# Other estimated times in the planner of a streaming encoder layer (attention and delta rule with two chains)

## The chip, the cores and the metric

The kernel runs on one core of a Trainium2 chip. The time is the device time of one execution in microseconds (us), the median of several runs. The core has a matrix engine (TensorE, PE in the profile, with its weight loads PEld), a vector engine (VectorE, DVE), an engine for functions of one argument (ScalarE, ACT), a general engine (GpSimd, POOL) and SyncE (SP), which issues the DMAs of this kernel. Each engine works off a queue of its own strictly in the order in which the program put instructions there. Engines tell each other of results through semaphores; an instruction whose input is not there yet holds up all that stands behind it in its queue.

## The reference

One layer of an encoder, for a prompt of 2048 frames and for a sample of 32 frames with caches. The width is 1024. In short:

```python
hp = layer_norm(x_prompt); hs = layer_norm(x_sample)
qa, ka, va, za, qkv_b, zb, a_b, b_b, gate_a, gate_b = split(h @ w_in)     # 1024 -> 6160 columns
# branch A: 8 heads of 64, softmax attention over the own chunk of 64 frames and the 8 before it, bias by distance
ya = (attention(qa, ka, va, rel_bias) * silu(za)) @ w_branch_a
# branch B: 8 heads of 64, depthwise causal conv of width 4 + silu on q, k, v; q and k of unit length
g, beta = -exp(a_log) * softplus(a_b + dt_bias), sigmoid(b_b)
for each chunk of 64 frames:                                              # chunked delta rule, float32
    m = (k * beta) @ k.T * decay * strictly_lower
    t_inv = inverse(eye + m);  u = t_inv @ (v * beta);  w = t_inv @ (k * beta * exp(gc))
    v_new = u - w @ s                                                     # s: state, 64 x 64 per head
    o = (q * exp(gc)) @ s + (q @ k.T * decay) @ v_new
    s = s * exp(g_last) + k_dec.T @ v_new
yb = (rms_norm(o) * silu(zb)) @ w_branch_b
y = layer_norm(ALPHA * h + (sigmoid(gate_a) * ya + sigmoid(gate_b) * yb) @ w_out)
```

Results are both outputs, the newest keys and values, the last rows before the conv, and the states.

## The kernel before, in words

**Stages.** The prompt is worked off in two halves of 1024 frames, the sample with the second. For each half the kernel runs a delta-rule phase (`phase_b`, line 776) and then an attention phase (`phase_a`, line 1425). After the second attention phase comes the merge (`merge`, line 2036) with the two branch projections, the output projection and the last norm.

**Projections.** The input projection is cut into 48 jobs of 128 columns, plus one for the decay inputs, once per half. A list (`all_jobs`, line 1907) fixes their order. `divide` (line 613) splits weights into two f16 parts (`whi`, `wlo`: ScalarE and GpSimd), and `multiply` (line 657) issues 24 matmuls for each block of up to 512 frames into one of two PSUM banks (`pj`). Each block is then evacuated by ScalarE or VectorE to where its phase wants it: `raw` for the conv of the delta rule, `vf`, `rhi`, `zs` for attention, `sig` (through `sig_dram`) for the merge gates. Merge-gate jobs depend on no phase. They stand between the others: `HEAD`, `FILL` and `TAIL` (lines 50 to 55) say how many at the start of a half, between the delta-rule jobs, and after them. Jobs of attention wait until their phase has been entered, and that happens once the delta-rule phase before it is done.

**The delta rule.** A block is eight chunks of two heads; a half has eight blocks (four pairs of heads, two blocks each), and the second half has one more for the sample. For each block there are the conv (VectorE, ScalarE), the decay matrices (`prep`), the system (`system`: products of keys and queries), the solution by forward substitution (`substitute`, line 1229: for each of 31 columns VectorE multiplies into `sys_t` and subtracts from `sys_u`), the inverse, and then the chain (`chain`, line 1305). The chain goes over the chunks one after the other because of the state. One chunk's step is: TensorE multiplies the state (`x`), VectorE forms `r`, TensorE multiplies by the inverse, VectorE forms `vn`, TensorE multiplies by the keys, VectorE forms the new `state`; two more matmuls make the output `o`. Every pair of heads has a chain of its own, and two of them can be under way at once (`x_banks = places(2)`, line 1291). `tail` (line 1337) norms the output and writes `gb` (`gs` for the sample).

**The planner.** Nothing of this is ordered by hand. Each piece of work is a Python generator, a stream, with a clock of its own, and `Flow` (line 155) always continues the stream whose clock is the earliest. When a stream issues an instruction, `Engine` (line 218) puts it in the engine's queue at once, asks `price` (line 224) for its estimated time, and `spend` (line 191) sets the stream's clock to

```python
t = max(t, self.busy.get(key, 0.0)) + cost
self.busy[key] = s.clock = t
```

where the first `t` is the clock plus a hop between engines (`HOP_PE, HOP, HOP_SAME = 0.1, 0.2, 0.12`, line 53: into TensorE, into another engine, and from an engine to itself). Buffers and banks are handed over through gates, at the planned clock, and the issue of DMAs has its place by the same clock. So the estimates decide the order of instructions in every queue, and nothing else: on the chip an instruction takes what it takes.

In `price`, key `"PE"` is TensorE, `"V"` VectorE, `"S"` ScalarE, `"G"` GpSimd; `n` is the number of elements per partition, `far` says that an operand lies in PSUM, and `more` counts operands that are themselves tensors of one value per partition. In the trace nearly all instructions stand at line 259, the helper that issues them, so the prediction goes by tiles.

Of the kernel before, what the change touches and what calls it, by code (L numbers as in the profile page):

```python
# [210 lines left out]
def width(ap):  # L211
    n = 1
    for k in ap.shape[1:]:
        n *= k
    return n


class Engine:
# [5 lines left out]
    def price(self, name, a, k):  # L224

        if self.key == "PE":
            n, m = width(a[2]), width(a[1])
            if name == "transpose":
                n = m = max(a[1].shape[0], m)
            if a[1].dtype == F16:  # L230
                return max(n / 2400.0, m / 4800.0)
            if a[1].dtype == F32R:
                return n / 2400.0
            return max(n, m) / (1200.0 if name == "transpose" else 600.0)
        ins = [k[x] for x in ("in_", "in0", "in1") if x in k] or list(a[1:2])
        out = k["out"] if "out" in k else a[0]
        n = width(ins[0] if name in ("bn_stats", "tensor_reduce") else out)
        far = any(getattr(x, "space", None) == PSUM for x in ins + [out])
        if self.key == "G":
            if k.get("op") == ALU.pow:  # L240
                return 0.55 + 0.125 * n
            return 0.03 + n / 1200.0 if name == "memset" else 0.1 + n / (960.0 if name == "affine_select" else 480.0)
        more = sum(not isinstance(k.get(x, 0.0), (int, float, type(None)))
                   for x in ("scale", "bias", "accum_out", "scalar1", "scalar2"))
        if self.key == "S":

            table = k.get("func") == AF.Ln
            if "func" in k and table != self.table and k["func"] != AF.Copy:
                self.table = table
                return 1.28 + self.price(name, a, k)  # L250
            return (0.05 if far else 0.093) + 0.093 * more + n / 1200.0
        fast = name in ("tensor_copy", "tensor_scalar") and not far
        return (0.125 if far else 0.068) + 0.06 * more * fast + n / (1920.0 if fast else 960.0)

    def __getattr__(self, name):
        f = getattr(self.eng, name)
# [2038 lines left out]
```

## Time and profile before

| | us |
|---|---|
| median of 3 runs | 2121.21 (2118.57 to 2124.31) |
| the profiled execution | 2124.96 |
| its span | 2123.1 |
| mean granted TensorE clock | 0.98 |

A row of a group names the tiles it writes and reads (`r<-x,negc,v_t`), shapes, the count, then the busy time, the mean of one instruction in ns, and the idle time of its engine just before. A row of the timeline starts with the time from the span's start and the duration. A row of the waits names who waited, for whom, and the total, the number and the longest. Where a plain float32 matmul is counted, the trace holds two records for each (264 of `x<-r,u_bd` for 132 of `r`). Matmuls overlap one another, so the record of one is longer than its share of the engine.

### The profile page before, as it was taken

Reading aid. Unit: us, or ns where it says so; the run is one execution under the profiler, and the core shown is the slowest. Engines: PE = TensorE matmul, PEld = TensorE weight load, DVE = VectorE, ACT = ScalarE, POOL = GpSimd, SP = SyncE. Lnnn points to the kernel's source line nnn. Section 1 sums busy time; section 2 is a strip of 40 time slices with the busy share of each in tenths; the row PEclk is TensorE's granted clock in tenths of the full one; section 3 lists DMA queues with packets and bytes.
Section 4 is the critical chain, followed back from the end, with each engine's and each line's share of the span. In section 5 each row is a group of like instructions: output and inputs, shape, how many; then the busy total and the mean of one; then the engine's idle time right before and its main releaser. Section 6 shows DMA issues by size and latency. Waiting matters only on the chain. (4 is left out here: it accounts for less than half of the span.)

```text
span 2123.1 us, 41363 instructions
## 1 busy us (share of the span) xinstructions
PE 1994.4 (94%) x15098; PEld 1422.5 (67%) x15098; DVE 1534.2 (72%) x4660; ACT 978.7 (46%) x2098; POOL 634.3 (30%) x708
## 2 busy tenths in 40 slices
PE   4999898999999999999899999999999988999998
PEld 4454665666465656666666676767776777988896
DVE  7689989884277768779898987347657667766676
ACT  5655544443465667564444443346656652111110
POOL 6243333232322122333233232310110223443343
PEclk9999999899999999999999999999999999999999
DMA  3223232222423233222223233332322435443331
GB/s 120 75 84 102 76 88 78 67 79 82 122 67 120 82 93 99 70 73 76 58 70 94 62 86 85 99 100 72 92 77 67 138 120 191 128 123 103 116 107 61
DMA packets 197719, 196.49 MB, mean 93 GB/s; under 512 B 79622, under 2 KB 147570, under 8 KB 197516
## 3 DMA queue, kind: packets, MB, share of 16 engines
q1 hardware_dynamic: 197516, 193.85, 30.9%
q8 instruction: 119, 1.95, 0.4%
q14 instruction: 84, 0.69, 0.1%
HBM read 135.91 MB, written 50.53 MB: 88 GB/s over the span
## 5 line engine op out<-in xcount | busy, mean ns | idle before, releaser
L259 PE MATMUL pj<-hi,whi 128*128 128x512 f16 (+2 forms) x1992 | 650.7, 342 | 8.6 <-POOL whi L259 3.0
L259 PE MATMUL pj<-hi,wlo 128*128 128x512 f16 (+2 forms) x1952 | 640.8, 341 | 0.4 <-POOL wlo L259 0.4
L259 PEld LDWEIGHTS <-whi 128*128 128x128 f16 x3984 | 416.0, 106 | 217.5 <-issue 11.2
L259 PE MATMUL pj<-lo,whi 128*128 128x512 f16 (+2 forms) x1992 | 461.9, 340 | 0.0
L259 POOL TENSOR_TENSOR wlo<-wraw,whi 128x512 f16<-128x512 f32 x192 | 228.6, 1193 | 630.1 <-ACT whi L259 345.1
L259 PEld LDWEIGHTS <-wlo 128*128 128x128 f16 x1952 | 205.5, 105 | 108.5 <-issue 8.9
L259 ACT CAST mh<-sg 128x256 fp32r<-128x256 f32 x64 | 25.9, 407 | 276.1 <-DVE sg L259 276.0
L259 DVE TENSOR_TENSOR sys_u<-sys_u,sys_t 128x60 f32<-128x60 f32 (+24 forms) x527 | 135.7, 258 | 18.2
L259 PE MATMUL a<-ghi,whi 128*128 128x256 f32 (+1 forms) x512 | 134.8, 293 | 7.1 <-DVE sg L259 6.8
L259 ACT ACTIVATE wraw<-wraw,w_scale 128x1024 f32<-128x1024 f32 (+1 forms) x98 | 111.4, 1137 | 59.2 <-DVE w_scale L259 57.1
L259 ACT CAST ph<-b 128x512 f16<-128x512 f32 (+2 forms) x224 | 92.6, 422 | 92.7 <-PE b L259 86.1
L259 PE MATMUL a<-ghi,wlo 128*128 128x256 f32 (+1 forms) x512 | 131.9, 287 | 0.0
L259 ACT CAST whi<-wraw 128x512 f16<-128x512 f32 (+1 forms) x196 | 119.4, 611 | 27.1 <-PE pj L259 24.2
L259 DVE TENSOR_TENSOR pl<-b,ph 128x512 f16<-128x512 f32 (+2 forms) x224 | 107.6, 484 | 28.9 <-ACT ph L259 28.0
L259 DVE TENSOR_TENSOR sys_t<-sys_u,sys_p 128x54 f32<-128x54 f32 (+21 forms) x459 | 123.6, 269 | 4.0
L259 ACT ACTIVATE sb<-sb,mx,unit 128x640 f32<-128x640 f32 (+4 forms) x128 | 109.0, 852 | 25.5 <-DVE mx L259 25.1
L259 DVE SCALAR_TENSOR_TENSOR acc<-raw,cwT,acc 128x512 f32<-128x512 f32 x144 | 113.2, 786 | 8.4 <-ACT acc L259 7.4
L259 POOL TENSOR_TENSOR w_scale<-w_scale,mhalf 128x1 f32<-128x1 f32 x49 | 31.0, 633 | 288.0 <-DVE w_scale L259 230.1
L259 PEld LDWEIGHTS a<-ghi,whi 128*128 128x128 f32 x512 | 99.3, 194 | 8.8 <-DVE sg L259 7.9
L259 PE MATMUL b<-ident,sb 128*128 128x128 f32 x560 | 98.8, 276 | 2.9 <-ACT tmp L259 0.6
L259 ACT COPY v_t<-o 128x64 f32<-128x64 f32 x132 | 27.5, 209 | 158.3 <-PE o L259 121.5
L259 PEld LDWEIGHTS a<-ghi,wlo 128*128 128x128 f32 x512 | 98.9, 193 | 0.4 <-DVE wlo L259 0.2
(350 smaller groups left out, 4238.9 us busy)
## 6 DMA issues: line engine op xcount, KB each, us to landing
wraw<-in_w_in SPq DMA_DIRECT2D x192, 256.0 KB
sg<-sig SPq DMA_DIRECT2D x112, 128.0 KB
sig<-sig SPq DMA_DIRECT2D x44, 256.0 KB
sys_p<-sol_p SPq DMA_DIRECT2D x17, 512.0 KB
x<-in_x_p SPq DMA_DIRECT2D x16, 512.0 KB
xt<-in_x_p SPq DMA_DIRECT2D x16, 512.0 KB
out_y_p<-xt SPq DMA_DIRECT2D x16, 512.0 KB
glo<-g SPq DMA_DIRECT2D x14, 512.0 KB
```

Source lines behind the costliest of these rows:

```text
L259: r = f(*a, **k)
```

## The change

The arithmetic of `price` is changed, and only that. On VectorE, ScalarE and GpSimd the constant part of every estimate grows: by 0.040 us, 0.050 us and 0.120 us (powers on GpSimd stay). On TensorE, f16 matmuls get a floor and a small constant, float32r matmuls a lower rate, plain float32 matmuls one fixed time (by the number of partitions of the stationary operand), and float32 transposes one of two fixed times. The hops, the DMA estimates, the job list and all instructions stay. The streams are therefore continued in another order, and the queues of all engines, SyncE's with its DMAs among them, get the same instructions in another order.

```diff
             if a[1].dtype == F16:
-                return max(n / 2400.0, m / 4800.0)
+                return max(0.029, n / 2400.0 + 0.0025)
             if a[1].dtype == F32R:
-                return n / 2400.0
-            return max(n, m) / (1200.0 if name == "transpose" else 600.0)
+                return n / 2265.0
+            if name == "transpose":
+                return 0.109 if n > 64 else 0.06
+            return 0.165 if a[1].shape[0] > 32 else 0.07
...
-            return 0.03 + n / 1200.0 if name == "memset" else 0.1 + n / (960.0 if name == "affine_select" else 480.0)
+            return 0.150 + n / 1200.0 if name == "memset" else 0.220 + n / (960.0 if name == "affine_select" else 480.0)
...
-            return (0.05 if far else 0.093) + 0.093 * more + n / 1200.0
+            return (0.100 if far else 0.143) + 0.093 * more + n / 1200.0
         fast = name in ("tensor_copy", "tensor_scalar") and not far
-        return (0.125 if far else 0.068) + 0.06 * more * fast + n / (1920.0 if fast else 960.0)
+        return (0.165 if far else 0.108) + 0.06 * more * fast + n / (1920.0 if fast else 960.0)
```

## The prediction

> **What bounds the kernel now.** I read the page first: engines, then the slices (40 equal pieces of the span, busy share in tenths).
>
> ```profile
> PE 1994.4 (94%) x15098; PEld 1422.5 (67%) x15098; DVE 1534.2 (72%) x4660; ACT 978.7 (46%) x2098; POOL 634.3 (30%) x708
> ...
> PE   4999898999999999999899999999999988999998
> ...
> DVE  7689989884277768779898987347657667766676
> ```
>
> TensorE is busy 94% of the span; 128.7 us are left (2123.1 - 1994.4). In the two stretches where VectorE's digits are mostly 8 and 9, the delta-rule phases (one per half of the prompt), TensorE's show 8 among the 9. The windows view cuts these stretches out, and others; its columns are length, then busy us (instructions) of PE, weight loads, DVE, ACT, POOL, then granted clock, DMA share, GB/s.
>
> ```profile
> 200.00:450.00 250.00, 230.44 (x1728) 156.40 (x1726) 222.49 (x782) 117.65 (x247) 83.11 (x110) 0.95 0.29 79
> 450.00:551.00 101.00, 98.64 (x688) 61.71 (x687) 47.12 (x194) 41.45 (x86) 31.61 (x30) 1.00 0.32 93
> 1000.00:1275.00 275.00, 250.97 (x2180) 187.37 (x2179) 243.20 (x845) 122.08 (x279) 85.51 (x124) 0.99 0.29 75
> 1275.00:1383.00 108.00, 103.89 (x839) 73.64 (x838) 53.78 (x219) 36.72 (x86) 28.85 (x26) 0.97 0.33 94
> ...
> 1710.00:1800.00 90.00, 76.86 (x549) 65.88 (x548) 64.14 (x131) 31.29 (x70) 29.17 (x25) 0.92 0.50 159
> ...
> 0.00:100.00 100.00, 68.28 (x402) 42.60 (x403) 70.07 (x175) 58.41 (x105) 44.71 (x56) 0.95 0.27 93
> ...
> 1500.00:1600.00 100.00, 98.53 (x921) 71.28 (x919) 64.17 (x232) 60.28 (x141) 11.58 (x10) 1.00 0.30 86
> ...
> 1800.00:1900.00 100.00, 100.00 (x666) 91.97 (x665) 70.01 (x114) 12.95 (x35) 44.16 (x33) 1.00 0.40 123
> ```
>
> Rows one and three are the heavy parts of the delta rule: VectorE busy 89% and 88%, TensorE 92% and 91%. Rows two and four are the ends of these phases: VectorE falls to 47% and 50%, and gate projections keep TensorE at 98% and 96%. Then the entry to the merge (13.1 us of TensorE idle), the start (31.7 us), attention (1.5 us in 100) and the merge (none).
>
> The view of waits, for the chain of the delta rule (r, vn and state are VectorE's three results of one chunk's step; columns: us in total, times, longest):
>
> ```profile
> PEld x L259 <- DVE r L259: 40.2, 82, 1.8
> PEld x L259 <- DVE vn L259: 36.1, 63, 1.8
> ...
> PEld x L259 <- DVE state L259: 21.4, 42, 2.6
> ```
>
> TensorE's queue comes to the next link of the chain before VectorE has delivered it: 187 waits, 97.7 us, 0.52 us each. A part is covered by matmuls in flight; behind each waiting weight load stands all the rest of TensorE's queue. Only another order can change these waits, and the diff changes orders.
>
> One more reading, the slack behind each delta-rule phase. Its end must come before the next attention phase's projections may leave PSUM; until then TensorE works off gate projections. VectorE's last outputs of the two phases (gb, gs) and ScalarE's first evacuations of attention (vf), from the timeline:
>
> ```profile
> 536.48 0.88 DVE L259 SCALAR_TENSOR_TENSOR gb<-b,gz,gb 128x256 f32<-128x256 f32 x2
> ...
> 550.83 0.69 ACT L259 ACTIVATE vf<-pj,w_inv 128x512 f32<-128x512 f32 x1 [0.97 <-PE pj L259]
> ...
> 1362.32 0.70 DVE L259 TENSOR_SCALAR gs<-gs,w_inv 64x32 f32<-64x32 f32 x4
> ...
> 1383.05 0.69 ACT L259 ACTIVATE vf<-pj,w_inv 128x512 f32<-128x512 f32 x1 [3.60 <-PE pj L259]
> ```
>
> From the end of gb (537.4) to 550.8 are 13.5 us, from the end of gs (1363.0) to 1383.05 are 20.0 us: together 33.5 us by which TensorE's waits may shrink before the end of the chain, and no longer TensorE, sets when attention starts.
>
> **The change part by part.** No instruction is added, removed or resized, so each engine's busy time stays. What moves is each queue's order, through the planner's clock.
>
> VectorE: every price rises by 0.040 us. Two neighbours with nothing in the way, two neighbours on ScalarE, and a case with GpSimd at work:
>
> ```profile
> 1346.37 0.28 DVE L259 TENSOR_SCALAR vn<-x,sc 128x64 f32<-128x64 f32 x1
> 1346.56 0.35 DVE L259 TENSOR_TENSOR ms<-ms 128x8 f32<-128x8 f32 x2
> ...
> 1367.71 0.48 ACT L259 ACTIVATE sig<-pj,w_half 128x272 f32<-128x272 f32 x1
> 1368.09 0.61 ACT L259 CAST whi<-wraw 128x512 f16<-128x512 f32 x1
> ...
> 355.23 1.04 POOL L259 TENSOR_TENSOR v_t<-v_t,ms 128x512 f32<-128x512 f32 x1 [0.16 <-DVE sys_t L259]
> 355.27 1.05 DVE L259 TENSOR_TENSOR sys_u<-sys_u,sys_t 128x30 f32<-128x30 f32 x1
> ...
> L259 DVE TENSOR_TENSOR sys_u<-sys_u,sys_t x527: 173/218/1214, 142.5 to 1323.9; 128x60 f32<-128x60 f32 x17, 128x28 f32<-128x28 f32 x14, 128x66 f32<-128x66 f32 x12, 128x48 f32<-128x48 f32 x11
> ...
> L259 DVE TENSOR_TENSOR sys_u<-sys_u,sys_t 128x60 f32<-128x60 f32 (+24 forms) x527 | 135.7, 258 | 18.2
> ```
>
> vn (64 columns from PSUM) holds VectorE for 0.19 us although its record is 0.28 us long. The old price is 0.125 + 64/960 = 0.192, the new one 0.232. So the old price is the spacing of undisturbed neighbours, and the new one lies between spacing and record. But sys_u, whose median record is 218 ns, takes 1.05 us beside a GpSimd instruction of 1.04 us, and its mean is 258 ns: 40 ns above the median, just what the diff adds. The new price is thus about the mean cost with such disturbances, spread evenly.
>
> The Trainium skill (Perfetto Trace Analysis, Optimizing Scalar/DVE Operations) gives about 60 ns (125 ns with PSUM) as VectorE's engine-busy overhead per instruction and 93 and 51 ns for ScalarE, and says that profiled latency is about twice that because half of it overlaps with the next instruction; vn agrees (0.19 against 0.28). By this rule the diff charges for time in which the engine is free, and the sum would come out slower; that is the second rival.
>
> ScalarE: +0.050 us. sig leaves after 0.38 us; old 0.05 + 0.093 + 272/1200 = 0.370, new 0.420. I cost this at nothing: in the heavy parts ScalarE is busy 47% and 44%, and its evacuations run beside the other bank's matmuls. Without that cover, (247 + 279) x 0.05 = 26 us of planned work would count. GpSimd: +0.120 us, 33% and 31% busy there, nothing likewise; 234 x 0.12 = 28 us uncovered.
>
> TensorE: f16 matmuls of 512 columns go from 0.213 to 0.216, float32r from 0.107 to 0.113 (256) and 0.213 to 0.226 (512). The merge's pieces of the chain that ended last give the true ones:
>
> ```profile
> 1833.78 22.81 PE a L259 x192
> ...
> 1862.38 5.45 PE b L259 x24
> ```
>
> 22.81/192 = 0.119 and 5.45/24 = 0.227: both new prices are nearer. But TensorE has no idle time in the merge, so a better estimate has nothing to remove there; the same holds for attention. The start I also take as unchanged: 0. Plain float32 matmuls of the chain fall from 0.213 to 0.165. What a round trip is really worth stands at the end of the first phase, where the chain runs alone on VectorE:
>
> ```profile
> 515.12 0.28 DVE L259 SCALAR_TENSOR_TENSOR r<-x,negc,v_t 128x64 f32<-128x64 f32 x1 [0.53 <-PE x L259]
> 515.93 0.28 DVE L259 TENSOR_SCALAR vn<-x,sc 128x64 f32<-128x64 f32 x1 [0.53 <-PE x L259]
> 516.75 0.28 DVE L259 SCALAR_TENSOR_TENSOR state<-state,sc,x 128x64 f32<-128x64 f32 x1 [0.53 <-PE x L259]
> ...
> L259 DVE SCALAR_TENSOR_TENSOR r<-x,negc,v_t 128x64 f32<-128x64 f32 x132 | 36.9, 279 | 25.5 <-PE x L259 23.8
> ```
>
> 0.81 us from one VectorE link to the next. The plan's round trip is hop 0.1 + matmul + hop 0.2 + VectorE: old 0.1 + 0.213 + 0.2 + 0.192 = 0.705, new 0.1 + 0.165 + 0.2 + 0.232 = 0.697. The unloaded chain is not repaired: 0.008 us worse. What is repaired is its queueing. The four delta-rule rows hold 782 + 194 + 845 + 219 = 2040 VectorE instructions; 132 chunk steps of three links are 396 of them, so 1644/396 = 4.15 others stand per link, and the plan's link comes up to 4.15 x 0.04 = 0.166 us later when all of them are ahead of it. Then TensorE's queue has that much other work before it reaches the link. Ends: none ahead, 187 waits x (-0.008) = 1.5 us lost; all ahead, 187 x (0.166 - 0.008) = 29.5 us won. I take half of them ahead (a link becomes ready at any point between its neighbours): 187 x (0.083 - 0.008) = 14 us. That is under the 33.5 us of slack, so it reaches the end.
>
> SyncE's queue is written by the same clock: a load issued behind a DMA that waits for a late result is late too. The longest waits of this kind now:
>
> ```profile
> POOL ms L259 <- DMA gb<-z: 15.4, 1, 15.4
> ...
> POOL wlo L259 <- DMA qd<-rhi: 13.0, 1, 13.0
> ```
>
> Both fall on GpSimd, which is idle 70% of the span; 0 in the sum, 15 us either way as its bound.
>
> Sum: the profiled execution took 2124.96 us (span 2123.1 and 1.9 around it). 2124.96 - 14 = 2111. It lay 3.75 us above the median of the runs shown (2121.21), so for the median I forecast **2107 us**.
>
> **The rivals.** First, the order hardly changes what happens: conv, delta-rule and gate projections come in a fixed list and wait for fixed numbers of buffers, and the unloaded round trip moves by 0.008 us. For it: VectorE at 89% sets the pace of the heavy parts whatever TensorE's order. Against it: the 187 waits are waits of order. Time 2121.
>
> Second, slower: the plan overcharges VectorE where it is fullest. Place: the heavy parts. Price: 782 x 0.04 = 31 us and 845 x 0.04 = 34 us by which the planned chain ends later, with gate projections set ahead of its links; the real TensorE then keeps the links back while VectorE idles. It decides where the chain's end comes later by more than the slack, 13.5 and 20.0 us; then TensorE has no gates left and idles until attention opens. At full price (31.3 - 13.5) + (33.8 - 20.0) = 31.6 us, at the point itself 0; the middle is 16: 2137. The rows of vn and sig speak for it, the mean of sys_u against it. It is what the skill's rule on overlapped overhead (same section) would bring about.
>
> Third, slower at one place: the entry to the merge (13.1 us of TensorE idle in 90) loses as much again, since there VectorE, GpSimd and half-busy DMA engines feed new weights in an order of their own: 2134. Against it: the prices there become truer.
>
> Fourth, a larger gain: links also come sooner for VectorE. Its idle time in the heavy parts is 27.5 + 31.8 = 59.3 us; half of that and the 14: 2121.2 - 44 = 2077. It needs the phases themselves to shorten.
>
> **How the numbers follow.** 0.3% is 6.4 us, about what a measurement of this kernel can tell from no change. Chances: forecast 0.40 (own range 2092 to 2123 by its two ends; 0.34 of it below 2114.8), no change 0.18, overcharge 0.25, merge entry 0.08, larger gain 0.09. Faster 0.34 + 0.09 = 0.43, same 0.06 + 0.18 = 0.24, slower 0.33. The range takes in the larger gain and most of the overcharge (full price 2153): 2074 to 2148.
>
> **What would show it.** Right: the three chain waits of TensorE's weight loads together well below 97.7 us (about 60 or less); VectorE's busy time and counts as before; TensorE idle in the heavy rows below 44 us (19.6 + 24.0 now); the slack behind each phase smaller than 13.5 and 20.0 but above zero; a lone round trip still 0.81 us. Wrong: chain waits as long as before (first rival); TensorE idle between the last gate projection and the first vf, with gb or gs ending later than now (second); the fifth row below 77 us of TensorE per 90 (third); VectorE above 92% in the heavy parts (fourth).

## The result, and the profile after

The changed kernel takes 2145.52 us (median of 4 runs, 2144.23 to 2152.01) against 2120.32 us before in the same comparison: a ratio of 1.0126 with a 95% interval of 1.011 to 1.0142. It is 25 us **slower**; I had forecast 2107, faster by 14. The profiled execution took 2152.01 us, 6.5 us above its median, with a span of 2149.8.

First the page of the changed kernel: engines, then the slices of TensorE and of its granted clock (tenths).

```profile
PE 2002.5 (93%) x15098; PEld 1451.1 (67%) x15098; DVE 1534.6 (71%) x4660; ACT 975.8 (45%) x2098; POOL 640.8 (30%) x708
...
PE   4999999999899998997999999899999998999998
...
PEclk8999999899899999999999999699999999999999
```

Counts are the same and VectorE's busy time is (1534.6 against 1534.2). TensorE's busy time grew by 8.1 us with the same 15098 matmuls, while its mean granted clock fell from 0.98 to 0.96, and one slice stands at 6. The waits of the chain, which were 187 and 97.7 us:

```profile
PEld x L261 <- DVE r L261: 26.7, 48, 3.1
...
PEld x L261 <- DVE vn L261: 19.3, 31, 1.7
...
PEld x L261 <- DVE state L261: 8.5, 24, 0.8
```

They are 103 and 54.5 us. What I forecast of TensorE's waits came about, and the time still rose. To see where it went, I cut both spans at the same events: ScalarE's first evacuation of the decay inputs (`ab`) of each half, its first evacuation of attention (`vf`) of each half, and the end of attention's last output (`ga`). So the rows are start, first delta rule, first attention, second delta rule, second attention, merge. The windows view of before:

```profile
0.00:75.40 75.40, 44.65 (x240) 31.12 (x241) 52.82 (x138) 37.47 (x75) 35.85 (x43) 0.93 0.29 102
75.40:550.80 475.40, 446.90 (x3087) 279.12 (x3086) 373.97 (x1252) 236.28 (x456) 163.92 (x205) 0.97 0.30 85
550.80:883.00 332.20, 325.36 (x2492) 199.46 (x2491) 228.03 (x777) 208.65 (x436) 78.06 (x85) 0.99 0.31 93
883.00:1383.00 500.00, 465.33 (x3818) 334.16 (x3817) 387.50 (x1296) 229.10 (x491) 155.09 (x214) 0.98 0.29 78
1383.00:1736.00 353.00, 344.03 (x3207) 249.09 (x3205) 224.82 (x780) 210.75 (x494) 50.59 (x44) 1.00 0.31 89
1736.00:2123.10 387.10, 368.18 (x2264) 329.51 (x2262) 267.03 (x418) 56.40 (x146) 150.82 (x119) 0.98 0.39 123
```

And of the changed kernel:

```profile
0.00:79.30 79.30, 47.46 (x240) 31.73 (x241) 52.21 (x138) 36.75 (x76) 35.88 (x43) 0.89 0.28 97
79.30:548.00 468.70, 443.21 (x3107) 285.80 (x3105) 369.24 (x1249) 240.30 (x462) 162.03 (x202) 0.96 0.30 85
548.00:889.40 341.40, 323.40 (x2469) 201.67 (x2470) 230.24 (x781) 203.09 (x430) 82.50 (x87) 0.98 0.31 91
889.40:1395.00 505.60, 472.35 (x3836) 352.12 (x3834) 384.84 (x1287) 228.77 (x493) 152.68 (x208) 0.94 0.27 75
1395.00:1761.00 366.00, 345.23 (x3154) 247.03 (x3154) 227.82 (x785) 211.11 (x495) 56.42 (x50) 0.98 0.30 88
1761.00:2149.80 388.80, 370.81 (x2295) 332.76 (x2295) 270.23 (x422) 55.79 (x147) 151.25 (x120) 0.98 0.38 122
```

The differences are +3.9, -6.7, +9.2, +5.6, +13.0 and +1.7 us, together the 26.7 us of the spans. The two delta-rule phases, on which my whole sum rested, come out level (-1.1 us). **Attention, which I had put at zero, is 22.2 us longer**, with 18.0 and 20.8 us of TensorE idle instead of 6.8 and 9.0.

How the delta-rule phases ended in the changed kernel (last gate evacuation `sig`, first evacuation of attention `vf`, VectorE's last outputs `gb` and `gs`):

```profile
525.35 0.69 ACT L261 ACTIVATE sig<-pj,w_half 128x512 f32<-128x512 f32 x1
...
548.01 1.26 ACT L261 ACTIVATE vf<-pj,w_inv 128x512 f32<-128x512 f32 x2
...
554.42 0.88 DVE L261 SCALAR_TENSOR_TENSOR gb<-b,gz,gb 128x256 f32<-128x256 f32 x2 [2.40 <-PE b L261]
...
1354.68 0.49 ACT L261 ACTIVATE sig<-pj,w_half 128x272 f32<-128x272 f32 x1
...
1391.97 0.70 DVE L261 TENSOR_SCALAR gs<-gs,w_inv 64x32 f32<-64x32 f32 x4
...
1394.98 1.05 ACT L261 ACTIVATE vf<-pj,w_inv 128x512 f32<-128x512 f32 x2
...
1400.85 0.88 DVE L261 SCALAR_TENSOR_TENSOR gb<-b,gz,gb 128x256 f32<-128x256 f32 x2 [2.27 <-PE b L261]
```

`gb` of the first phase and `gs` of the second end 17.9 us (555.3 against 537.4) and 29.7 us (1392.7 against 1363.0) later. In the second phase the last prompt block now ends behind the sample: its `gb` ends at 1401.7 us, where that of before ended at 1356.0. The gates are used up 22 and 40 us before attention begins. And attention does not begin after these last outputs, but about 7 us before they end: `vf` stands in ScalarE's queue behind the chain's last copies (of `o` into `v_t`, at 546.73 and 1394.20 us). In the first of the two holes TensorE still had attention's first projections, until about 541 us. What became of it in the second, in windows of the changed kernel, and a piece of its timeline there:

```profile
1355.00:1375.00 20.00, 17.88 (x159) 16.13 (x155) 4.77 (x18) 4.93 (x18) 0.00 (x0) 0.71 0.13 38
1375.00:1395.00 20.00, 17.94 (x80) 16.03 (x79) 8.04 (x35) 2.46 (x10) 1.62 (x2) 0.50 0.03 4
1395.00:1405.00 10.00, 5.31 (x27) 3.93 (x28) 2.43 (x9) 2.06 (x4) 6.47 (x6) 0.54 0.24 59
...
1366.23 0.63 PE L261 MATMUL x<-r,u_bd 128*128 128x64 f32 x2
1366.66 0.63 PE L261 MATMUL x<-vn,kd_bd 128*128 128x64 f32 x2
1367.09 0.64 PE L261 MATMUL o<-state,q_bd 128*128 128x64 f32 x2
1367.51 0.63 PE L261 MATMUL o<-vn,qk_bd 128*128 128x64 f32 x2
```

The last prompt block and the sample run their chains here side by side (until about 1382 us, then the prompt block goes on alone), from about 1361 us with no projections between. The granted clock falls to 0.50, and in the piece shown the chains' matmuls follow each other every 0.43 us with no gap: at half the clock two chains fill TensorE's records. Before, the lone chain's end was mixed with projections, the granted clock was 1.00, and the next matmul came 0.17 us after one of these:

```profile
515.95 0.33 PE L259 MATMUL o<-state,q_bd 128*128 128x64 f32 x2
516.12 0.38 PE L259 MATMUL pj<-hi,whi 128*128 128x512 f16 x1
```

The Trainium skill (TensorE: Matmul & The Clock Gate, Part 1) says that TensorE's clock drops to half after an idle window of about 3.4 us and comes back after as long a busy one. The halving agrees (0.50). An idle window of that length is not to be seen here: the longest gap between TensorE's records is 1.1 us in the 20 us before the clock falls (at about 1363 us) and 0.46 us from there to 1394 us, and the clock stays at 0.50. The ends of these records are modelled, so whether the matrix engine rested between them is not shown.

### The profile page after: what moved, and what is told of

The parts are those of the page before. It is cut to its first block, busy times and chain, and to the rows that moved or that the text cites. A ratio compares the mean times of both kernels' runs of the same rounds, so it can differ in the third digit from the quotient of the medians.

```text
span 2149.8 us, 41400 instructions
## 1 busy us (share of the span) xinstructions
PE 2002.5 (93%) x15098; PEld 1451.1 (67%) x15098; DVE 1534.6 (71%) x4660; ACT 975.8 (45%) x2098; POOL 640.8 (30%) x708
## 5 line engine op out<-in xcount | busy, mean ns | idle before, releaser
L261 PE MATMUL pj<-hi,whi 128*128 128x512 f16 (+2 forms) x1992 | 659.0, 346 | 23.9 <-ACT raw L261 8.7
L261 PE MATMUL pj<-hi,wlo 128*128 128x512 f16 (+2 forms) x1952 | 649.0, 345 | 3.1 <-POOL wlo L261 3.1
L261 PE MATMUL pj<-lo,whi 128*128 128x512 f16 (+2 forms) x1992 | 451.8, 338 | 0.3 <-POOL lo L261 0.3
L261 DVE TENSOR_TENSOR sys_t<-sys_u,sys_p 128x54 f32<-128x54 f32 (+20 forms) x459 | 120.9, 263 | 3.5
L261 DVE SCALAR_TENSOR_TENSOR acc<-raw,cwT,acc 128x512 f32<-128x512 f32 x144 | 112.6, 782 | 9.6 <-ACT acc L261 8.5
```

The costliest lines, as they stand in the source:

```text
L261: r = f(*a, **k)
```

## The experiments

Three theories at the start. **Overcharge**: VectorE's dearer estimate is the harmful part, as in my second rival. **The hole**: the loss is the uncovered end of the chain. **Luck**: any change of the estimates is another draw of the order, and before is a good one. All times below are medians; ratios are to before in the same comparison.

### One part of the change alone

```diff
e1  -        return (0.125 if far else 0.068) + ...     VectorE's line alone
    +        return (0.165 if far else 0.108) + ...
e2  TensorE's lines alone
e3  ScalarE's and GpSimd's lines alone
```

> Only VectorE's estimates grow by 0.040 us; the other estimates are those of before. Overcharge theory (the second rival): VectorE is the engine whose queue is fullest in the delta rule, so this part carries the loss: +15 to +30 us against before, and the second half's last delta-rule output (gs) ends 10 us or more after the last gate projection. Theory of luck (any change of the estimates draws another order, and the ends of the phases fall where they fall): anything between -15 and +25 us, with no relation to the other parts. Theory that the float32 price of TensorE did it: within 5 us of before.

> Only TensorE's estimates change. Overcharge theory: within 6 us of before, the two solutions of the last delta-rule systems end near 1292 and 1324 us as before. Float32 theory (the plain float32 price falls from 0.213 to 0.165, so TensorE's queue comes to the chain's links too early): +15 us or more. Theory of luck: anything between -15 and +25 us.

> Only ScalarE's (+0.050 us) and GpSimd's (+0.120 us) estimates grow. Overcharge theory: at most a third of the loss, 0 to +8 us, since both are under half busy in the delta rule. Theory of luck: anything between -15 and +25 us.

Measured: VectorE alone 2138.01 us, 1.0096 (1.0068 to 1.0123); TensorE alone 2121.38, 1.0009 (0.9995 to 1.0023); ScalarE and GpSimd alone 2141.57, 1.0106 (1.008 to 1.0133). The float32 price is cleared by itself; e2 even shortens the chain's waits from 97.7 to 75.4 us, and the time does not follow. e1 fits the overcharge theory: +18 us, and `gs` ends 28 us after the last gate (1391.8 against 1363.8). e3 does not: overcharge would have left it under 8 us, and it cost 22. In e3 the gates last until 5 and 7 us before attention, and the loss stands first of all in the first delta-rule phase (487.8 us against 475.4). And the parts don't add: 0.96 + 0.09 + 1.06 = 2.1%, where all together cost 1.26%.

### Filling the second hole

```diff
-HEAD, TAIL = [2, 3], [6, 6]
+HEAD, TAIL = [2, 3], [6, 8]        (on the changed kernel)
```

> The changed kernel, with eight instead of six gate jobs after the delta-rule jobs of the second half (the two come from the end of the last attention phase). Theory that the hole does it (the gates run out at 1355 us and the last chain runs until 1391 us without cover): two jobs are about 21 us of matmuls, they fill the hole, and the time falls by 8 to 20 us, to 2126 to 2137. If the loss lies elsewhere (attention order, start), it falls by less than 4 us, or rises because the last attention phase misses its own filler.

2140.83 us, 1.0112 (1.0085 to 1.0138): the interval overlaps the changed kernel's. Windows of this run, the former hole, then the second delta rule and the second attention:

```profile
1355.00:1375.00 20.00, 17.95 (x179) 16.51 (x179) 5.52 (x21) 6.64 (x21) 1.16 (x1) 0.83 0.21 65
1375.00:1396.00 21.00, 21.00 (x161) 15.70 (x161) 9.78 (x39) 6.59 (x17) 7.02 (x7) 1.00 0.22 68
888.00:1396.00 508.00, 476.54 (x3956) 352.98 (x3955) 386.95 (x1294) 235.78 (x505) 159.16 (x214) 0.96 0.28 79
1396.00:1761.00 365.00, 337.41 (x3066) 241.27 (x3063) 224.56 (x781) 203.34 (x482) 49.96 (x45) 0.97 0.29 83
```

The hole is filled and the clock is back at 1.00 in its second half, but the phase is not shorter: `gs` ends 4.8 us sooner, at 1387.9 us, the last gate now leaves at 1392.2, and the first `vf`, at 1396.0, waits for its projection behind the gates. And attention, which lost two gate jobs, lasts 365.0 us as with them (366.0), with 27.6 us idle. So the hole is not what the kernel pays for, and attention there is not held by TensorE's load.

### The size and the sign of VectorE's estimate, and its place

```diff
e5  +        return (0.127 if far else 0.070) + ...     +0.002
e6  +        return (0.095 if far else 0.038) + ...     -0.030
e7  +0.040 only while an attention phase is the current one
e8  +0.040 only while a delta-rule phase is the current one
```

> VectorE's estimates of before grow by 0.002 us, a twentieth of the change: too little to be truer or less true, but enough to draw another order. Overcharge theory: within 4 us of before. Theory of luck (the order of before is a good draw, another draw costs some us to some tens of us): a difference of 5 to 25 us, probably slower.

> VectorE's estimates of before fall by 0.030 us, below the measured spacing of undisturbed neighbours. Overcharge theory (the more VectorE is charged the slower): the same as before or faster, 2095 to 2122. Theory of luck, or a theory by which the prices of before are the true ones and every departure costs: slower by 10 to 30 us, 2130 to 2150.

> VectorE's +0.040 us counts only while the planner is in the attention phases (from the entry of each until the next delta-rule phase, or the last stage); in the delta-rule phases the prices of before hold. Theory of attention (the +13 us and +16 us by which the two attention phases of the VectorE-only run were longer): each attention phase longer by 10 us or more, 2138 to 2150 in all. My own step (attention is TensorE's, nothing moves): 2120.

> The counterpart: VectorE's +0.040 us only in the delta-rule phases. Theory of attention: the first attention phase within 4 us of 332, the total between 2095 and 2125 (the VectorE-only run had its first delta-rule phase 10 us longer and its second 26 us shorter). Overcharge theory as in my second rival (the delta rule's tail runs out of gates): 2135 to 2150.

e5: 2131.31 us, 1.0045 (1.0023 to 1.0067). Two nanoseconds, which make no estimate truer, cost 0.45%. e6: 2168.69, 1.0224 (1.019 to 1.0258): undercharging costs more than the change did, against the overcharge theory, and more than the 2150 us at most that the other theories gave. e7: 2129.87, 1.0032 (1.0013 to 1.0051), with attention phases of 332.4 and 359.7 us; e8: 2120.00, 0.9995 (0.9979 to 1.0011), with 335.2 and 364.8 us. Around before (five draws, shown below) these phases last 330.3 to 336.3 and 353.1 to 360.9 us. So dearer VectorE in attention lengthens neither, and the theory of attention's own price, which gave 2138 us or more, falls. A lengthening by a few us is not excluded: e7's profiled execution was the fastest of its ten, 9.0 us below their median. Dearer VectorE in the delta rule lengthens the second attention phase, which itself was planned with the old prices (to 364.8 us, and to 365.0 in e17 and e18 below, which have the same dearer VectorE): there it is **the order that the delta rule leaves behind**. The first attention phase lengthens only where VectorE is dearer in both places (345.7 us in e1). The two places cost 0.3% and nothing, both together (e1) 1.0%. e8 is also the second rival put to the test in its own place, the delta rule. There the gates run out 40 and 19 us before attention, and the time is that of before, not the 2135 to 2150 us of the overcharge theory: gates that run out early do not by themselves make the kernel slower.

The chain's waits and the second delta-rule phase follow VectorE's estimate as my mechanism says: at -0.030 us 112.6 us of waits and a phase of 520.5 us, at 0 97.7 and 500.0, at +0.040 (e1) 65.4 and 474.3. The first delta-rule phase does not: 490.7, 475.4, 485.9. And the changed kernel itself, with the same +0.040, has 54.5 us of waits and yet a second phase of 505.6 us.

### The hop into TensorE

```diff
-HOP_PE, HOP, HOP_SAME = 0.1, 0.2, 0.12
+HOP_PE, HOP, HOP_SAME = 0.2, 0.2, 0.12
```

> The prices of before, with the hop into TensorE 0.2 instead of 0.1 us: it closes the gap that I named between the plan's round trip of the lone chain (0.705 us) and the measured one (0.81 us), which the diff left open. If the latency of the chain is what the plan lacks: TensorE's waits for r, vn and state fall from 97.7 us to under 70 us and the time by 5 to 20 us. If not (or if luck rules): 2120 to 2145.

2144.72 us, 1.0114 (1.0094 to 1.0135). The chain's waits of this run:

```profile
PEld x L259 <- DVE r L259: 47.8, 85, 5.3
...
PEld x L259 <- DVE vn L259: 30.2, 62, 2.1
...
PEld x L259 <- DVE state L259: 19.4, 47, 1.8
```

97.4 us, unchanged. Closing the gap of the unloaded round trip (0.705 planned, 0.81 measured) helps neither the waits nor the time; that reading of mine was a number without consequence.

### Neighbours: is it the estimates or the draw?

VectorE's estimate is moved by 0.002 and 0.004 us up and down, around before and around the changed kernel.

```diff
e9  (0.123 ... 0.066)   e13 (0.129 ... 0.072)   e14 (0.121 ... 0.064)     the rest as before
e10 (0.167 ... 0.110)   e11 (0.163 ... 0.106)   e15 (0.169 ... 0.112)   e16 (0.161 ... 0.104)     the rest as changed
```

> The prices of before with VectorE's 0.002 us lower: a second neighbour of before, as free of meaning as the one 0.002 us above it (which was 0.45% slower). Theory of luck alone: before is itself one draw out of many, its neighbours lie 0 to 1.2% above it. Theory that truer prices order better: the neighbours of before lie within 0.6% of it, well below the changed kernel's 1.26%.

> The changed kernel with VectorE's estimates 0.002 us higher still: a neighbour of it. Theory of luck alone: as likely to be near the neighbours of before (0 to 0.6% above before) as near the changed kernel. Theory that the fitted prices order worse by themselves: 0.8 to 1.8% above before, like the changed kernel.

> The changed kernel with VectorE's estimates 0.002 us lower. The same two expectations as for the neighbour above: 0 to 0.6% above before if it was the draw, 0.8 to 1.8% if the fitted prices themselves order worse.

> The prices of before, VectorE's 0.004 us higher: one more neighbour of before. Two theories for the changed kernel's 1.26%. Luck alone: neighbours of before and of after come from one heap, and some of before lie over 1%. Fitted prices order worse: neighbours of before stay under 0.8%, neighbours of after over it in most cases.

> The prices of before, VectorE's 0.004 us lower. As for the neighbour 0.004 us higher: under 0.8% above before if the fitted prices are worse by themselves, anywhere between -0.5 and +1.7% by luck alone.

> The changed kernel, VectorE's estimates 0.004 us higher. Fitted prices worse by themselves: 0.8 to 1.8% above before. Luck alone: as likely 0 to 0.6%.

> The changed kernel, VectorE's estimates 0.004 us lower. Fitted prices worse by themselves: 0.8 to 1.8% above before. Luck alone: as likely 0 to 0.6%.

| VectorE's shift | around before | around the changed kernel |
|---|---|---|
| -0.004 us | 1.0086 (1.0047 to 1.0125) | 1.0082 (1.0048 to 1.0116) |
| -0.002 us | 1.0055 (1.0036 to 1.0074) | 1.0168 (1.0136 to 1.0200) |
| none | 1 | 1.0126 (1.0110 to 1.0142) |
| +0.002 us | 1.0045 (1.0023 to 1.0067) | 1.0066 (1.0043 to 1.0089) |
| +0.004 us | 1.0022 (1.0005 to 1.0040) | 1.0050 (1.0031 to 1.0070) |

All four neighbours of before are slower than before: it is the best draw of its five. The means are 0.42% and 0.98%; their difference, 0.57%, has an interval of about -0.04 to 1.18% when the five draws of each column are taken as its spread. So of the 1.26% about 0.4 is the luck of before, about 0.6 probably the estimates, and the rest the changed kernel's own draw; that the fitted estimates order worse by themselves is likely, not shown. Neither theory's terms were met in full: one neighbour of before lies above 0.8%, but none over 1%, and two of the four around the changed kernel lie below 0.8%. Nor is it known why before is a good draw: no run varies the job list (`HEAD`, `FILL`, `TAIL`) around before, so that list may suit the order of before better than others.

The stages, as means over the five profiles of each column, show more than the totals:

| mean of five, us | start | delta 1 | attention 1 | delta 2 | attention 2 | merge | chain waits |
|---|---|---|---|---|---|---|---|
| around before | 77.8 | 471.5 | 333.1 | 503.3 | 357.2 | 385.8 | 96.5 |
| around changed | 78.6 | 479.8 | 341.5 | 487.0 | 366.1 | 385.7 | 58.7 |

Chain waits lie at 90.5 to 100.2 us in one column and at 54.5 to 62.2 in the other; the first attention phase at 330.3 to 336.3 and 338.3 to 344.5, the second at 353.1 to 360.9 and 362.8 to 369.0. These three don't overlap: they belong to the estimates, not to the draw. Each of these rows rests on one execution per draw, 8.0 us below to 6.5 us above the median of its kernel. The delta-rule phases vary from draw to draw by 10 to 26 us within a column. In the second of them the changed kernel is the exception: it has 505.6 us, its four neighbours 480.8 to 484.8, and the five draws around before 498.7 to 508.7. So around the changed kernel this phase is shorter, except in the draw that was measured as the change.

### Filling the first hole, and a combination

```diff
e17  e8 (VectorE +0.040 in the delta rule only), and TAIL = [9, 6]
e18  e8, and TensorE's lines of the change
```

> VectorE's +0.040 us in the delta-rule phases only (2120 us, level with before), and nine instead of six gate jobs after the delta-rule jobs of the first half. In the run without them the gates ran out 40 us before the first attention phase began. Theory that running out is what costs the attention phases: the ramp from the first evacuation of attention to its first scores falls from 39 to 37 or 38 us as in before, TensorE's granted clock in the first delta-rule phase rises from 0.951 to 0.97 or more, the first attention phase is 8 us or more shorter than 335, and the total falls to 2105 to 2115. If the attention phases are held up by their own order: the phase stays within 4 us of 335, total 2115 to 2125.

> TensorE's fitted estimates (level with before by themselves, the last attention phase 5 us shorter) together with VectorE's +0.040 us in the delta-rule phases only (level with before, the second delta-rule phase 21 us shorter). If parts add up: 2105 to 2118, faster than before. If each combination is a new draw, as the parts of the change were (0.1 and 1.0 and 1.1% against 1.26% for all): 2120 to 2140.

e17: 2118.94 us, 0.9986 (0.9974 to 0.9997). Windows of e8, its first attention phase; then of e17, the 20 us before its first attention phase begins and that phase:

```profile
551.00:886.00 335.00, 323.00 (x2470) 197.97 (x2471) 229.56 (x781) 205.04 (x431) 82.06 (x86) 0.98 0.31 91
```

```profile
551.00:571.00 20.00, 18.71 (x90) 8.57 (x88) 3.47 (x14) 7.21 (x13) 11.53 (x11) 1.00 0.40 122
571.00:871.00 300.00, 290.43 (x2317) 183.32 (x2318) 214.36 (x747) 192.22 (x411) 68.01 (x73) 0.99 0.31 90
```

The three gate jobs moved: the first delta-rule phase grew by 20 us and attention shrank by 35 (335.0 to 300.0, with 153 fewer records of matmuls), but the second delta-rule phase grew by 17 (479.4 to 496.8). The theory of running out gave 2105 to 2115 us; the time missed that. The ramp, from the first evacuation of attention to the first matmul of its scores, is 35.7 us instead of 39.6 in e8; in e4 it fell from 45.2 to 40.0 us at the second attention phase, where before had 41.1. On the mean of five draws the ramps are 38.1 and 41.1 us around before, 40.0 and 45.6 around the changed kernel. So 1.9 and 4.5 us of ramp, with the clock low, stand in the 8.4 and 8.9 us by which the attention phases are longer, and gates at the end of the delta rule take this ramp away. But e4 took it away and its second attention phase, with two gate jobs fewer, was as long as without: that the ramp is what lengthens the phase is not shown. The cause stays open, and so does why the shorter first attention phase was paid back in the next delta-rule phase.

e18: 2113.69 us, 0.9965 (0.9945 to 0.9986), chain waits 51.2 us: faster than both kernels, near the gain I had expected of the change, although its gates run out 25 us before each attention phase. Since two nanoseconds move the time by 0.5%, I don't take it for the merit of these two parts.

## Why the prediction was wrong, point by point

- **Counts and busy time stay**: right for VectorE (1534.6 against 1534.2 us); TensorE's busy time rose by 8.1 us, at a lower granted clock.
- **Chain waits fall**: right in kind, and more than forecast. They fell by 43 us (to "about 60 or less": 54.5), and by 38 us on the mean of five. The sum had taken 14 us off them, while the sign asked for some 38: the two did not belong together. TensorE's idle time in the heavy rows is below the 44 us named: the same windows of the changed kernel (200 to 450 and 1000 to 1275 us) have 15.0 and 14.3.
- **"That is under the 33.5 us of slack, so it reaches the end"**: this step failed. I held the end of the chain fixed and let TensorE's waits shrink before it, each us of wait a us of time. The waits were replaced by projections, taken earlier; `gb` and `gs` ended 17.9 and 29.7 us later, the gates ran out 22 and 40 us before attention, and TensorE's idle time went to the ends of the phases: it fell by 14.3 us in the heavy rows, but over the whole phases only from 28.5 to 25.5 and from 34.7 to 33.3 us. The delta-rule phases together gained 1.1 us of the 14. Other runs show the same: e2, e8 and e17 have 22 to 33 us less of chain waits than before, and their times differ from it by +0.09, -0.05 and -0.14%. The slack was not what I took it for, either. The last outputs do not open attention: in the changed kernel `vf` leaves 7 us before the last `gb` ends, behind the chain's last copies on ScalarE.
- **Attention 0**: failed: +9.2 and +13.0 us, the largest term. I argued that a phase with TensorE at 98% has nothing to win, and so put at nothing what another order could lose there: TensorE's idle time in the two phases went from 15.8 to 38.8 us. VectorE's estimates in attention alone are not the cause (e7, up to a few us). For the second phase it is the order that the delta rule leaves behind (e8); about half of it shows as a longer ramp, but in e4 the phase was not shorter without that. For the first phase the cause stays open.
- **Start and merge 0**: +3.9 and +1.7 us; over five draws +0.8 and -0.1.
- **SyncE's order, ScalarE and GpSimd at nothing**: the last is wrong. Their estimates alone cost 22 us (e3), by another order, though neither engine is busy half of the time in the delta rule.
- **The rivals**: the second one came nearest (2137, at most 2153; measured 2145.52). That is luck of the number. Its point of decision, gates used up before the chain ends, is what the trace shows, but e8 and e18 show the same and are level with before and faster. Its price did not fall where I put it: the second delta rule is 16 us shorter, not longer, on the mean of five, and the loss stands in attention and in the first delta rule (8.4, 8.9 and 8.3 us). "The order hardly changes what happens" was false, the merge's entry did not move, and the larger gain did not come.
- **The range** held the time (2074 to 2148), for a reason that it did not contain: a term for drawing the order anew, which the neighbours put at up to 0.9% around before and a spread of 1.2% around the changed kernel.

## What to carry to other kernels

Where an order comes from estimated times, compare draws before judging an estimate: move it by an amount that means nothing, and take a change for real only where it stands clear of these neighbours. A wait removed from the fullest queue is not yet time gained: follow the work that takes its place to the end of its stage, and into the start of the next, and count the idle time of the whole stage. And a stage that runs at 98% is not safe from a change of order: it has little to win and much to lose (the second attention phase, 353.1 us before, took 345.6 us at best, in e12, and 369.0 at worst).

## What the runs showed of the hardware

- A chain of small float32 matmuls without other work between them lets TensorE's clock fall to half although TensorE's records (with modelled ends) show no gap over 0.5 us: granted 0.50 over 20 us with 17.94 us busy, one matmul every 0.43 us, where 0.17 us were seen at full clock. Projections between the links are cover in this sense too: with two gate jobs in that place (e4) the same window had 0.83 and 1.00.
- VectorE's subtraction of 30 columns took 1.05 us beside a GpSimd instruction of 1.04 us, against a median of 0.218 us over all 527 of these subtractions. Of the 527, the 370 that ran with no GpSimd instruction beside them took 0.24 us at most; 32 others took more than 0.5 us and make up the 40 ns between median and mean. So the 40 ns that the diff adds fall on a few instructions, and a plan that spreads them evenly did not order better.
